# Merging the blocks of a chunk inverse with zero-masked operands on all 128 rows

## The chip, the cores and the metric

The kernel runs on one core of one Trainium2 chip. The metric is the device time of one execution in microseconds; the time of the kernel before is the median of three runs.

## The reference

Two layers of a block over 512 tokens (256 of context, 256 latent): neighbourhood attention and a gated delta rule side by side, then an MLP. The part that matters here belongs to the delta rule. For each chunk, head and direction a unit lower triangular matrix is inverted:

```python
kb = kc * bc[..., None]
a = jnp.where(strict, jnp.einsum('nbhid,nbhjd->nbhij', kb, kc) * decay, 0.0)
tinv = unit_lower_inverse(a)          # (I + a)^-1
u = tinv @ (vc * bc[..., None])
w = tinv @ (kb * eg[..., None])
...                                   # then a scan over the chunks
```

The reference uses chunks of 64 tokens; the kernel works with tiles of 128 tokens, which gives the same recurrence. A layer then has 4 tiles t, 2 directions d and 4 heads: 32 matrices of 128x128, numbered n = 8t + 4d + h.

## The kernel before

Each layer first computes projections and gates, then the inversion and the scan (`mixer`), then the output projection and the MLP. Products of weights are made of three matmuls each (lines 274 to 276), with the weights split into two parts by ScalarE (`whi`, line 248) and VectorE (`wlo`, line 250).

The strings `ord0` and `ord1` list the pieces of work of a layer; at the X stands the inversion with the scan behind it. The pieces named after the X (attention `a`, lines 696 to 719; projections N, K, Q, Z; the steps `f` of the modulation, line 301) are independent of the inversion. Outside the first stage, which is ordered by hand, a planner decides how the instructions of all pieces are laid on each engine, so that attention and projection matmuls stand between those of the inversion. Each engine then works in that order.

The inversion of a layer goes like this. Lines 809 to 816 make the 32 matrices in `U` (128 partitions, 32 matrices, 128 columns), for each tile t from a product `kk` on TensorE and a decay factor from ScalarE (line 805). Lines 823 and 824 take the four diagonal blocks of 32x32 of every matrix out of `U` and transpose them into `MT`, one block row of 32 partitions at a time. Lines 825 to 833 invert the diagonal blocks by substitution on VectorE, all at once, in `Y`. Line 834 transposes the result, lines 835 and 836 scatter it into `XT`, which has been cleared by GpSimd (line 795), and lines 837 and 838 scatter the other orientation into `U`.

Then come two levels of merging, for each half t2 of 16 matrices (two tiles t). The first level joins pairs of 32x32 blocks to 64x64 blocks: p1 (line 849, tiles of 32x32 in the array, once for each r), copied to `y1` by ScalarE (line 850), then pz (lines 853 and 854), whose results are negated into `U` by VectorE (855) and into `XT` by ScalarE (856). The second level joins the two 64x64 blocks to 128x128: p2 (line 862), copied to `y2` (864), then p3 (867 and 868), negated into `U` (869) or `XT` (870); direction 1 is scaled into `U` at line 871. The contraction of each of these matmuls runs over the 32 or 64 partitions of one block:

```python
for r in range(2):
    for n in range(16):
        PE.matmul(p1[B_[r], n], U[A_[r], n0 + n, B_[r]], XT[A_[r], n0 + n, A_[r]], ...)
    S.activation(y1[B_[r]], p1[B_[r]], AF.Copy)
```

The PSUM tiles of this work come from a ring of three (`sm`), the working tiles in SBUF from a ring of seven (`tr`).

Of the kernel before, what the change touches and what calls it, by code (L numbers as in the profile page):

```python
# [11 lines left out]
F32 = mybir.dt.float32  # L12
# [3 lines left out]
AF = mybir.ActivationFunctionType  # L16
ALU = mybir.AluOpType
AX = mybir.AxisListType
# [158 lines left out]
def body(ctx, tc, a, out, dump=None):  # L177
    nc = tc.nc
    V, S, G, PE, SP = nc.vector, nc.scalar, nc.gpsimd, nc.tensor, nc.sync
    dump = dump or (lambda name, ap: None)  # L180

    P0 = ctx.enter_context(tc.tile_pool(name="P0", bufs=1))
# [5 lines left out]
    def sm(name):  # L188
        return PP.tile([128, 512], F32, name=name, tag="g", bufs=CFG["g"])
# [6 lines left out]
    ident = cst[:, C_ID:C_ID + 128]  # L196
# [6 lines left out]
    mh = P0.tile([128, 8], F32, name="mh")  # L203
    V.memset(mh, -0.5)

    hsel = P0.tile([128, 4], F32, name="hsel")
    tdf = P0.tile([128, 8], F32, name="tdf")
    tdsel = P0.tile([128, 8], F32R, name="tdsel")
# [4 lines left out]
    def late_const():  # L213
        SP.dma_start(cst[:, 128:], a["const"][:, 128:])
        V.tensor_copy(idb, ident)
        r = wraw(None)
        SP.dma_start(r[:, :384], a["masks"])
        V.tensor_copy(mb.rearrange("p a b -> p (a b)"), r[:, :384])
        V.tensor_reduce(hsel, ident.rearrange("p (j c) -> p c j", c=4), axis=AX.X, op=ALU.add)
        t = small([128, 32], "t32", bufs=1)  # L220
        V.tensor_reduce(t, ident.rearrange("p (j c) -> p j c", c=4), axis=AX.X, op=ALU.add)
        V.tensor_reduce(tdf, t.rearrange("p (u c) -> p c u", c=8), axis=AX.X, op=ALU.add)
        V.tensor_copy(tdsel, tdf)

    def small(shape, name, dt=F32, bufs=3):
        return P0.tile(shape, dt, name=name, tag="sm_" + name, bufs=bufs)
# [6 lines left out]
    def wraw(src, name="wraw"):  # L233
        r = P0.tile([128, 1024], F32, name=name, tag="wraw", bufs=4)
        if src is not None:
            r_dma[:] = [SP.dma_start(r, src).ins]
        return r
# [229 lines left out]
    def mixer(l, hT, pre, ctx_m):  # L467
# [3 lines left out]
        M = ctx_m.enter_context(tc.tile_pool(name="mix%d" % l, bufs=1, reuse_waits="tile"))  # L471

        def tr(name, shape=(128, 512), dt=F32, bufs=None):
            return M.tile(list(shape), dt, name=name, tag="tr", bufs=CFG["tr"])
# [8 lines left out]
        U = M.tile([128, 32, 128], F32, name="U", tag="U")  # L483
        XT = M.tile([128, 32, 128], F32, name="XT", tag="XT")
# [106 lines left out]
        beta = g = po = gc = gx = gt = cd = eg = ngc = gcb = neg = kd = None  # L591
# [205 lines left out]
        def decay(t, d, form, bias):  # L797
            pr = sm("gcr").rearrange("p (h c) -> p h c", h=4)
            m = mb[:, "abc".index(form)].unsqueeze(1).to_broadcast([128, 4, 128])
            PE.matmul(pr, idb, m, start=True, stop=False, skip_group_check=True)  # L800
            PE.matmul(pr, tdsel[:, 2 * t + d:2 * t + d + 1].to_broadcast([128, 128]), gx,
                      start=False, stop=True, skip_group_check=True)
            D_ = tr("dec").rearrange("p (h c) -> p h c", h=4)
            for h in range(H):
                S.activation(D_[:, h], pr[:, h], AF.Exp, bias=bias[:, t, 4 * d + h:4 * d + h + 1],
                             scale=-1.0 if form == "c" else 1.0)
            return D_

        for t in ts:
            kk_ = sm("kk").rearrange("p (h c) -> p h c", h=4)  # L810
            for h in range(H):
                kt_ = kqT[h][:, 0, 128 * t:128 * t + 128]
                PE.matmul(kk_[:, h], kt_, kt_, start=True, stop=True)
            for d in range(2):
                D_ = decay(t, d, "a" if d == 0 else "c", gcb)
                V.tensor_tensor(U[:, 8 * t + 4 * d:8 * t + 4 * d + 4], D_, kk_, op=ALU.mult)

        if l == 0:
            dump("U", U)
        q4 = [slice(32 * b, 32 * b + 32) for b in range(4)]  # L820
        MY = M.tile([128, 2, 32, 32], F32, name="MY", tag="my")
        MT, Y = MY[:, 0], MY[:, 1]
        for b in range(4):
            V.transpose(MT[q4[b]], U[q4[b], :, q4[b]].rearrange("p n i -> p i n"))
        S.activation(Y, MT, AF.Copy, scale=-1.0)
        V.memset(Y.rearrange("p a b -> p (a b)")[:, 0:1024:33], 1.0)
        for j in range(1, 31):
# [3 lines left out]
            V.tensor_tensor(tv, MT[:, j + 1:, j:j + 1].to_broadcast([128, m, j]),  # L831
                            Y[:, j:j + 1, 0:j].to_broadcast([128, m, j]), op=ALU.mult)
            V.tensor_tensor(Y[:, j + 1:, 0:j], Y[:, j + 1:, 0:j], tv, op=ALU.subtract)
        V.transpose(MT, Y.rearrange("p i j -> p j i"))
        for b in range(4):
            S.activation(XT[q4[b], :, q4[b]].rearrange("p n i -> p i n"), MT[q4[b]], AF.Copy)  # L836
        for b in range(4):
            V.transpose(U[q4[b], :, q4[b]].rearrange("p n i -> p i n"), Y[q4[b]])

        LT = U  # L840
        for t2 in range(2):
            n0 = 16 * t2
            y1 = tr("y1").rearrange("p (n c) -> p n c", n=16)
            p1 = sm("p1").rearrange("p (n c) -> p n c", n=16)
            pz = sm("pz").rearrange("p (n c) -> p n c", n=16)
            A_, B_ = [slice(64 * r, 64 * r + 32) for r in range(2)], [slice(64 * r + 32, 64 * r + 64) for r in range(2)]
            for r in range(2):
                for n in range(16):
                    PE.matmul(p1[B_[r], n], U[A_[r], n0 + n, B_[r]], XT[A_[r], n0 + n, A_[r]], start=True, stop=True)
                S.activation(y1[B_[r]], p1[B_[r]], AF.Copy)  # L850
            for r in range(2):
                for n in range(16):
                    PE.matmul(pz[A_[r], n], y1[B_[r], n], U[B_[r], n0 + n, B_[r]], start=True, stop=True)
                    PE.matmul(pz[B_[r], n], U[B_[r], n0 + n, B_[r]], y1[B_[r], n], start=True, stop=True)
                V.tensor_scalar(U[A_[r], n0:n0 + 16, B_[r]], pz[A_[r]], -1.0, None, op0=ALU.mult)
                S.activation(XT[B_[r], n0:n0 + 16, A_[r]], pz[B_[r]], AF.Copy, scale=-1.0)
            lo_, hi_ = slice(0, 64), slice(64, 128)
            for t in (2 * t2, 2 * t2 + 1):
                n0 = 8 * t
                p2 = sm("p2").rearrange("p (n c) -> p n c", n=8)  # L860
                for n in range(8):
                    PE.matmul(p2[hi_, n], U[lo_, n0 + n, hi_], XT[lo_, n0 + n, lo_], start=True, stop=True)
                y2 = tr("y2").rearrange("p (n c) -> p n c", n=8)
                S.activation(y2[hi_], p2[hi_], AF.Copy)
                p3 = sm("p3").rearrange("p (n c) -> p n c", n=8)
                for n in range(4):
                    PE.matmul(p3[lo_, n], y2[hi_, n], U[hi_, n0 + n, hi_], start=True, stop=True)
                    PE.matmul(p3[hi_, 4 + n], U[hi_, n0 + 4 + n, hi_], y2[hi_, 4 + n], start=True, stop=True)
                V.tensor_scalar(U[lo_, n0:n0 + 4, hi_], p3[lo_, 0:4], -1.0, None, op0=ALU.mult)
                S.activation(XT[hi_, n0 + 4:n0 + 8, lo_], p3[hi_, 4:8], AF.Copy, scale=-1.0)  # L870
                V.tensor_tensor(U[:, n0 + 4:n0 + 8], XT[:, n0 + 4:n0 + 8],
                                beta[:, t, 4:8].unsqueeze(2).to_broadcast([128, 4, 128]), op=ALU.mult)
        if l == 0:
            dump("LT", U)

# [182 lines left out]
    with tc.tile_pool(name="xin", bufs=1, reuse_waits="tile") as XP, \  # L1058
# [30 lines left out]
        with tc.manual_schedule(engines={nc.tensor.engine}):  # L1089
            for c in CFG["start"]:  # L1090
                i = cnt.get(c, 0)
                cnt[c] = i + 1
                part = range(KPART * i, KPART * (i + 1))
# [20 lines left out]
                else:  # L1114
                    first_block(pre[int(c)], part)
    fetch()
    late_const()
    P0.tile([128, 40], F32, name="pad")
    dump("h0", hT[0].bitcast(F32))
    x1d = P_dram.tile([256, 1024], F32, name="x1d")  # L1120
    for l in range(L):
        with ExitStack() as ctx_m:
            mT = mixer(l, hT, pre, ctx_m)
# [189 lines left out]
```

## Time and profile before

| what | us |
|---|---|
| median of 3 runs | 1299.35 |
| lowest, highest | 1298.74, 1306.26 |
| the profiled execution | 1304.05 |
| its span | 1302.3 |
| TensorE busy in the span | 1234.8 |
| VectorE busy | 875.1 |
| ScalarE busy | 604.6 |

PE is TensorE, PEld its loads of the stationary operand, DVE VectorE, ACT ScalarE, POOL GpSimd. The span runs from the first to the last instruction of the profiled execution. A busy TensorE can run at either of two clocks; the granted clock is given as a share of 2.4 GHz.

### The profile page before, as it was taken

The numbers are of one execution on the slowest core, as the hardware profiler recorded it, in microseconds if no ns is written. First come the engines' busy times: TensorE is split into PE (matmuls) and PEld (weight loads), VectorE is DVE, ScalarE is ACT, GpSimd is POOL, SyncE is SP. The second block draws the span as 40 slices with busy tenths as digits, with TensorE's granted clock in tenths as the row PEclk, the third lists the DMA queues.
The fourth block names the chain that finished last, engine by engine and source line by source line (L and its number), as shares of the span: only waits on it lengthen the run. The fifth ranks groups of instructions, "written<-read, shape, count | busy, mean of one in ns | idle before, by whom it ended". The sixth has DMA issues, their size and how long they took to land.

```text
span 1302.3 us, 20475 instructions
## 1 busy us (share of the span) xinstructions
PE 1234.8 (95%) x7976; PEld 1006.3 (77%) x7976; DVE 875.1 (67%) x1681; ACT 604.6 (46%) x1079; POOL 81.6 (6%) x82
## 2 busy tenths in 40 slices
PE   7999998999999999999999999899979998999997
PEld 3676666988878988777788888675669877788996
DVE  3788695466579955344444488897965668866677
ACT  2554545565555732322322455555454655544552
POOL 0212100001001000000000001221000010000000
PEclk9999995899999999999999999999958999899999
DMA  9613661023255643533532256235720256555552
GB/s 329 213 65 102 211 219 46 17 78 117 79 194 182 225 150 109 165 130 115 164 129 99 97 178 204 72 107 191 235 92 14 85 179 231 199 184 191 186 187 98
DMA packets 62721, 190.93 MB, mean 147 GB/s; under 512 B 7808, under 2 KB 17824, under 8 KB 62624
## 3 DMA queue, kind: packets, MB, share of 16 engines
q1 hardware_dynamic: 62624, 189.62, 44.2%
q8 instruction: 63, 1.03, 0.3%
q14 instruction: 34, 0.28, 0.1%
HBM read 187.46 MB, written 2.13 MB: 146 GB/s over the span
## 4 chain that ended last, share of the span: by engine, by line
PE 71%; DVE 11%; ACT 4%; issue 2%; POOL 1%; DMA 1%; DVEq 0%; ACTq 0%; POOLq 0%
PE pst L274 7%; PE pst L276 7%; PE pst L275 7%; PE pm L274 7%; PE pm L276 7%; PE pm L275 7%; PE pss L716 3%; PE adaps L301 2%; DVE wlo L250 2%; PE pss L696 2%; PE pss L713 2%; PE psn L274 1%; PE psn L275 1%; PE psn L276 1%; ACT XT L836 1%
## 5 line engine op out<-in xcount | busy, mean ns | idle before, releaser
L250 DVE TENSOR_TENSOR wlo<-wraw,whi 128x1024 fp32r<-128x1024 f32 x224 | 274.7, 1228 | 184.7 <-ACT whi L248 184.3
L248 ACT ACTIVATE whi<-wraw 128x1024 fp32r<-128x1024 f32 x224 | 237.0, 1060 | 316.6 <-PE pst L276 168.9
L274 PE MATMUL pm<-hhi,whi 128*128 128x256 f32 (+1 forms) x544 | 176.4, 324 | 0.8 <-ACT whi L248 0.7
L276 PE MATMUL pm<-hhi,wlo 128*128 128x256 f32 (+1 forms) x544 | 174.5, 321 | 0.0
L275 PE MATMUL pm<-hlo,whi 128*128 128x256 f32 (+1 forms) x544 | 174.4, 321 | 0.0
L274 PE MATMUL pst<-whi,ah 128*128 128x512 f32 x384 | 150.0, 391 | 0.0
L275 PE MATMUL pst<-wlo,ah 128*128 128x512 f32 x384 | 149.5, 389 | 0.0
L276 PE MATMUL pst<-whi,al 128*128 128x512 f32 x384 | 149.1, 389 | 0.0
L274 PEld LDWEIGHTS pm<-hhi,whi 128*128 128x128 f32 x544 | 103.5, 190 | 14.4 <-issue 5.8
L276 PEld LDWEIGHTS pm<-hhi,wlo 128*128 128x128 f32 x544 | 103.6, 190 | 7.7
L275 PEld LDWEIGHTS pm<-hlo,whi 128*128 128x128 f32 x544 | 103.6, 190 | 7.3
L274 PEld LDWEIGHTS pst<-whi,ah 128*128 128x128 f32 x384 | 72.1, 188 | 15.6 <-issue 0.8
L276 PEld LDWEIGHTS pst<-whi,al 128*128 128x128 f32 x384 | 72.1, 188 | 14.8
L275 PEld LDWEIGHTS pst<-wlo,ah 128*128 128x128 f32 x384 | 72.1, 188 | 14.7
L274 PE MATMUL psg<-hhi,whi 128*128 128x512 f32 (+1 forms) x216 | 78.2, 363 | 4.6 <-ACT XT L529 2.3
L276 PE MATMUL psg<-hhi,wlo 128*128 128x512 f32 (+1 forms) x216 | 78.0, 362 | 0.2 <-DVE wlo L250 0.2
L275 PE MATMUL psg<-hlo,whi 128*128 128x512 f32 (+1 forms) x216 | 77.8, 361 | 0.0
L531 DVE SCALAR_TENSOR_TENSOR XT<-U,cw,XT 128x512 f32<-128x512 f32 (+1 forms) x96 | 66.9, 728 | 0.5 <-ACT XT L529 0.4
L1191 ACT ACTIVATE ah<-mr 128x256 fp32r<-128x256 f32 (+1 forms) x68 | 33.5, 492 | 65.6 <-DVE mr L1189 65.6
L301 PE MATMUL adaps<-wraw,scT 128*32 128x256 f32 x640 | 56.0, 397 | 4.8 <-DMA wraw<-w_ada 4.6
L229 POOL TENSOR_TENSOR rs<-ve,mh 128x1 f32<-128x1 f32 x12 | 12.5, 1044 | 629.3 <-DVE bmv L394 362.2
L1192 DVE TENSOR_TENSOR al<-mr,ah 128x256 fp32r<-128x256 f32 (+1 forms) x68 | 35.2, 518 | 24.3 <-ACT ah L1191 24.2
(659 smaller groups left out, 2467.4 us busy)
## 6 DMA issues: line engine op xcount, KB each, us to landing
wraw<-w SPq DMA_DIRECT2D x140, 512.0 KB
wraw<-w_ada SPq DMA_DIRECT2D x80, 512.0 KB
wraw<-w_gdn SPq DMA_DIRECT2D x27, 512.0 KB
wraw<-w_out SPq DMA_DIRECT2D x24, 512.0 KB
xa<-w_ada SPq DMA_DIRECT2D x32, 256.0 KB
wraw<-w_vz SPq DMA_DIRECT2D x16, 512.0 KB
wraw<-w_na SPq DMA_DIRECT2D x16, 512.0 KB
lnrow<-lnr SPq DMA_DIRECT2D x8, 512.0 KB
```

The costliest lines, as they stand in the source:

```text
L248: S.activation(hi, r, AF.Copy)
L250: V.tensor_tensor(lo, r, hi.bitcast(F32), op=ALU.subtract)
L274: PE.matmul(o, l[0], r[0], start=start, stop=False)
L275: PE.matmul(o, l[0], r[1], start=False, stop=False)
L276: last_mm[:] = [PE.matmul(o, l[1], r[0], start=False, stop=stop).ins]
L301: PE.matmul(st["ps"][32 * g:32 * g + 32, :256], scT[:, k, :], w[:, 256 * g:256 * g + 256], start=(k == 0), stop=(k == 7), tile_position=(0 ...
L531: V.scalar_tensor_tensor(av, cin[:, sg:, kk:kk + 256], cw[:, b, kk:kk + 1], av, op0=ALU.mult, op1=ALU.add)
L696: PE.matmul(ps[:, :128 * nkt], nqT[hp][:, a2, qs], nkT[hp][i][:, a2, :128 * nkt], start=i == 0, stop=i == 1)
L713: PE.transpose(ps[:, 128 * kt_:128 * kt_ + 128], p_[:, 128 * kt_:128 * kt_ + 128], ident)
L716: PE.matmul(ps[:, 0:65], p_[:, 128 * kt_:128 * kt_ + 128], nv[:, kt_, hd], start=kt_ == 0, stop=kt_ == nkt - 1)
L1191: S.activation(ah, r, AF.Copy)
L1192: V.tensor_tensor(al, r, ah.bitcast(F32), op=ALU.subtract)
```

## The change

The diagonal blocks are gathered by ScalarE into `Y` as soon as the tile t that they belong to has been made, 16 copies a layer of 32 partitions by 256 elements; one transpose on all 128 partitions then makes `MT`. After the substitution the inverses stay compact: `low` is the transposed result in the layout (128, 32 matrices, 32 columns) and `upp` the other orientation.

A mask `keep` (one column for each block row of 32 partitions) makes zeros. `lowz` is `low` with all but one block row cleared, for each half and r; `y1` is the copied p1 with all but one block row cleared, in two versions. With these operands p1, pz, p2 and p3 contract over all 128 partitions; the foreign rows are multiplied by zeros. p1 has tiles of 128x64 in the array, pz of 128x32, p2 and p3 of 128x64. pz computes only the results that are used later: three of four for each matrix. The compact inverses are copied into `XT` and `U` piece by piece between the merging steps (`put_low`, `put_upp`, `put_rest`), and the steps of the two halves stand interleaved in the program. For p3 GpSimd clears the lower half of `y2`.

```diff
+        V.tensor_reduce(keep, ident.rearrange("p (b j) -> p b j", b=4), axis=AX.X, op=ALU.add)
...
         for t in ts:
...
+            for b in range(4):
+                S.activation(Y[q4[b], :, 8 * t:8 * t + 8].rearrange("p i n -> p n i"), U[q4[b], 8 * t:8 * t + 8, q4[b]], AF.Copy)
...
-        for b in range(4):
-            V.transpose(MT[q4[b]], U[q4[b], :, q4[b]].rearrange("p n i -> p i n"))
+        V.transpose(MT, Y)
         S.activation(Y, MT, AF.Copy, scale=-1.0)
...
-        V.transpose(MT, Y.rearrange("p i j -> p j i"))
-        for b in range(4):
-            S.activation(XT[q4[b], :, q4[b]].rearrange("p n i -> p i n"), MT[q4[b]], AF.Copy)
-        for b in range(4):
-            V.transpose(U[q4[b], :, q4[b]].rearrange("p n i -> p i n"), Y[q4[b]])
+        low = MT
+        V.transpose(low.rearrange("p n j -> p j n"), Y.rearrange("p i j -> p j i"))
+        lowz = {}
+        for t2 in range(2):
+            for r in range(2):
+                z = lowz[t2, r] = tr("lowz").rearrange("p (n c) -> p n c", n=16)
+                if t2 == 0:
+                    V.tensor_scalar(z, low[:, 0:16], keep[:, 2 * r:2 * r + 1], None, op0=ALU.mult)
+                else:
+                    S.activation(z, low[:, 16:32], AF.Copy, scale=keep[:, 2 * r:2 * r + 1])
+        upp = M.tile([128, 32, 32], F32, name="upp", tag="upp")
+        V.transpose(upp.rearrange("p n i -> p i n"), Y)
...
+        def merge_p1(t2):
+            n0 = 16 * t2
+            p1 = sm("p1").rearrange("p (n c) -> p n c", n=16)
+            for n in range(16):
+                for r in range(2):
+                    PE.matmul(p1[half[r], n], U[:, n0 + n, half[r]], lowz[t2, r][:, n], start=True, stop=True)
+            y1[t2] = [tr("y1").rearrange("p (n c) -> p n c", n=16) for _ in range(2)]
+            S.activation(y1[t2][0], p1, AF.Copy, scale=keep[:, 1:2])
+            V.tensor_scalar(y1[t2][1], p1, keep[:, 3:4], None, op0=ALU.mult)
+
+        def put_low(t2):
+            for b in (0, 1):
+                S.activation(XT[q4[b], 16 * t2:16 * t2 + 16, q4[b]], low[q4[b], 16 * t2:16 * t2 + 16], AF.Copy)
+
+        def put_upp(t2):
+            for b in (2, 3):
+                V.tensor_copy(U[q4[b], 16 * t2:16 * t2 + 16, q4[b]], upp[q4[b], 16 * t2:16 * t2 + 16])
+
+        def put_rest(t):
+            for b in (2, 3):
+                S.activation(XT[q4[b], 8 * t + 4:8 * t + 8, q4[b]], low[q4[b], 8 * t + 4:8 * t + 8], AF.Copy)
+            for b in (0, 1):
+                V.tensor_copy(U[q4[b], 8 * t:8 * t + 4, q4[b]], upp[q4[b], 8 * t:8 * t + 4])
+
+        def merge_pz(t2):
...
+            for n in range(16):
+                d = n // 4 % 2
+                for r in range(2):
+                    y, u = y1[t2][r][:, n], upp[:, n0 + n]
+                    if r == 1 or d == 0:
+                        PE.matmul(pz[q4[2 * r], n], y, u, start=True, stop=True, tile_position=(0, 64 * r))
+                    if r == 0 or d == 1:
+                        PE.matmul(pz[q4[2 * r + 1], n], u, y, start=True, stop=True, tile_position=(0, 64 * r + 32))
...
+        def merge_p2(t):
...
+                PE.matmul(p2[hi_, n], U[:, n0 + n, hi_], XT[:, n0 + n, lo_], start=True, stop=True)
+            y2[t] = tr("y2").rearrange("p (n c) -> p n c", n=8)
+            G.memset(y2[t][lo_], 0.0)
+            S.activation(y2[t][hi_], p2[hi_], AF.Copy)
+
+        def merge_p3(t):
...
+            for n in range(4):
+                PE.matmul(p3[lo_, n], y2[t][:, n], U[:, n0 + n, hi_], start=True, stop=True)
+                PE.matmul(p3[hi_, 4 + n], U[:, n0 + 4 + n, hi_], y2[t][:, 4 + n], start=True, stop=True)
...
+        for part, i in ((merge_p1, 0), (merge_p1, 1), (put_low, 0), (put_upp, 0), (merge_pz, 0), (put_low, 1), (put_upp, 1), (merge_pz, 1),
+                        (merge_p2, 0), (merge_p2, 1), (put_rest, 0), (merge_p3, 0), (put_rest, 1), (merge_p2, 2), (merge_p3, 1),
+                        (put_rest, 2), (merge_p2, 3), (merge_p3, 2), (put_rest, 3), (merge_p3, 3)):
+            part(i)
```

## Rows read from the trace of the kernel before

**Rows 1.** The page: busy time of the engines; the granted clock by slice

```profile
PE 1234.8 (95%) x7976; PEld 1006.3 (77%) x7976; DVE 875.1 (67%) x1681; ACT 604.6 (46%) x1079; POOL 81.6 (6%) x82
...
PEclk9999995899999999999999999999958999899999
```

**Rows 2.** Windows by stage, both layers: busy time (instructions) by engine, clock, DMA

```profile
core 0: us, PE busy (x) PEld busy (x) DVE busy (x) ACT busy (x) POOL busy (x), PEclk, DMA share, GB/s
134.00:151.00 17.00, 17.00 (x109) 11.58 (x108) 10.24 (x23) 12.40 (x40) 2.22 (x1) 1.00 0.63 201
...
194.00:204.00 10.00, 5.58 (x57) 3.10 (x55) 9.91 (x6) 8.94 (x7) 0.00 (x0) 0.75 0.35 118
198.96:233.10 34.14, 30.75 (x413) 25.37 (x409) 16.38 (x29) 16.25 (x24) 0.00 (x0) 0.50 0.15 48
236.50:240.00 3.50, 3.50 (x33) 2.66 (x32) 1.13 (x6) 1.59 (x4) 0.00 (x0) 0.51 0.00 0
...
944.70:954.70 10.00, 3.04 (x55) 1.94 (x53) 9.90 (x6) 9.16 (x8) 0.00 (x0) 0.76 0.54 185
949.92:984.05 34.13, 28.85 (x392) 24.63 (x390) 17.92 (x33) 15.76 (x23) 1.83 (x1) 0.50 0.12 40
...
153.50:156.60 3.10, 3.10 (x38) 1.53 (x37) 3.09 (x2) 1.20 (x2) 0.00 (x0) 1.00 0.43 96
```

**Rows 3.** Waits of TensorE, 196 to 250 us and 945 to 1000 us

```profile
PE p L849 <- ACT y L850: 3.4, 1, 3.4
PE p L849 <- ACT XT L836: 1.5, 1, 1.5
...
PE p L849 <- ACT y L850: 5.3, 1, 5.3
PE p L849 <- ACT XT L836: 2.3, 1, 2.3
```

**Rows 4.** Timeline, layer 0, VectorE and ScalarE: start, duration, instruction [idle before]

```profile
150.97 8.09 DVE L824 STREAM_TRANSPOSE MY<-U 32x1024 f32<-32x1024 f32 x4
...
193.80 2.10 DVE L834 STREAM_TRANSPOSE MY<-MY 128x1024 f32<-128x1024 f32 x1
195.82 7.72 DVE L838 STREAM_TRANSPOSE U<-MY 32x1024 f32<-32x1024 f32 x4
...
195.99 7.85 ACT L836 ACTIVATE XT<-MY 32x1024 f32<-32x1024 f32 x4 [0.98 <-DVE MY L834]
```

**Rows 5.** Timeline of TensorE: equal work at the low and the full clock

```profile
223.08 1.91 PE L849 MATMUL p<-XT,U 32*32 32x32 f32 x32
...
948.81 1.19 PE L849 MATMUL p<-XT,U 32*32 32x32 f32 x32 [2.26 <-ACT XT L836]
...
209.31 0.63 PE L275 MATMUL psn<-hlo,whi 128*128 128x512 f32 x1
209.74 0.63 PE L276 MATMUL psn<-hhi,wlo 128*128 128x512 f32 x1
...
187.69 0.39 PE L275 MATMUL psn<-hlo,whi 128*128 128x512 f32 x1
187.92 0.39 PE L276 MATMUL psn<-hhi,wlo 128*128 128x512 f32 x1
```

**Rows 6.** Groups of TensorE by form, 198.96 to 239.96 us: busy, mean ns

```profile
L853 PE MATMUL pz<-U,y 32*32 32x32 f32 x128 | 6.9, 225 | 0.0
L854 PE MATMUL pz<-y,U 32*32 32x32 f32 x128 | 6.9, 225 | 0.0
L862 PE MATMUL p<-XT,U 64*64 64x64 f32 x59 | 6.4, 288 | 0.0
L849 PE MATMUL p<-XT,U 32*32 32x32 f32 x104 | 6.2, 234 | 3.4 <-ACT y L850 3.4
...
L867 PE MATMUL p<-U,y 64*64 64x64 f32 x24 | 3.3, 318 | 0.0
```

**Rows 7.** Groups by line, the whole span: forms near the added ones

```profile
L413 DVE TENSOR_SCALAR x<-x,rs,nm 128x512 f32<-128x512 f32 x10 | 5.4, 544 | 0.1
...
L870 ACT ACTIVATE XT<-p 64x256 f32<-64x256 f32 x8 | 3.0, 375 | 0.8 <-DVE U L869 0.7
```

More of the change, by code (lines that the diff above doesn't have):

```diff
@@ L204, in body @@
     V.memset(mh, -0.5)
+    keep = P0.tile([128, 4], F32, name="keep")
     hsel = P0.tile([128, 4], F32, name="hsel")
@@ L807, in decay @@
             return D_
+        q4 = [slice(32 * b, 32 * b + 32) for b in range(4)]
+        MY = M.tile([128, 2, 32, 32], F32, name="MY", tag="my")
+        MT, Y = MY[:, 0], MY[:, 1]
         for t in ts:
@@ L816, in mixer @@
                 V.tensor_tensor(U[:, 8 * t + 4 * d:8 * t + 4 * d + 4], D_, kk_, op=ALU.mult)
+            for b in range(4):
+                S.activation(Y[q4[b], :, 8 * t:8 * t + 8].rearrange("p i n -> p n i"), U[q4[b], 8 * t:8 * t + 8, q4[b]], AF.Copy)
         if l == 0:
             dump("U", U)
-        q4 = [slice(32 * b, 32 * b + 32) for b in range(4)]
-        MY = M.tile([128, 2, 32, 32], F32, name="MY", tag="my")
-        MT, Y = MY[:, 0], MY[:, 1]
-        for b in range(4):
-            V.transpose(MT[q4[b]], U[q4[b], :, q4[b]].rearrange("p n i -> p i n"))
+        V.transpose(MT, Y)
         S.activation(Y, MT, AF.Copy, scale=-1.0)
@@ L840, in mixer @@
         LT = U
-        for t2 in range(2):
+        half = [slice(0, 64), slice(64, 128)]
+        lo_, hi_ = half
+        y1, y2 = {}, {}
+        def merge_p1(t2):
             n0 = 16 * t2
-            y1 = tr("y1").rearrange("p (n c) -> p n c", n=16)
             p1 = sm("p1").rearrange("p (n c) -> p n c", n=16)
-            pz = sm("pz").rearrange("p (n c) -> p n c", n=16)
[L846 to L872, printed above, removed]
@@ new lines, in put_upp @@
+        def put_upp(t2):
[8 more added lines that the diff above has]
+            n0 = 16 * t2
+            pz = sm("pz").rearrange("p (n c) -> p n c", n=16)
+            for n in range(16):
[6 more added lines that the diff above has]
+                        PE.matmul(pz[q4[2 * r + 1], n], u, y, start=True, stop=True, tile_position=(0, 64 * r + 32))
+            S.activation(XT[q4[1], n0:n0 + 16, q4[0]], pz[q4[1]], AF.Copy, scale=-1.0)
+            V.tensor_scalar(U[q4[2], n0:n0 + 16, q4[3]], pz[q4[2]], -1.0, None, op0=ALU.mult)
+            for t in range(2):
+                ns = slice(n0 + 8 * t, n0 + 8 * t + 4)
+                V.tensor_scalar(U[q4[0], ns, q4[1]], pz[q4[0], 8 * t:8 * t + 4], -1.0, None, op0=ALU.mult)
+                ns = slice(n0 + 8 * t + 4, n0 + 8 * t + 8)
+                S.activation(XT[q4[3], ns, q4[2]], pz[q4[3], 8 * t + 4:8 * t + 8], AF.Copy, scale=-1.0)
@@ new lines, in merge_p2 @@
+        def merge_p2(t):
+            n0 = 8 * t
+            p2 = sm("p2").rearrange("p (n c) -> p n c", n=8)
+            for n in range(8):
+                PE.matmul(p2[hi_, n], U[:, n0 + n, hi_], XT[:, n0 + n, lo_], start=True, stop=True)
[3 more added lines that the diff above has]
+        def merge_p3(t):
+            n0 = 8 * t
+            p3 = sm("p3").rearrange("p (n c) -> p n c", n=8)
+            for n in range(4):
+                PE.matmul(p3[lo_, n], y2[t][:, n], U[:, n0 + n, hi_], start=True, stop=True)
+                PE.matmul(p3[hi_, 4 + n], U[:, n0 + 4 + n, hi_], y2[t][:, 4 + n], start=True, stop=True)
+            V.tensor_scalar(U[lo_, n0:n0 + 4, hi_], p3[lo_, 0:4], -1.0, None, op0=ALU.mult)
+            S.activation(XT[hi_, n0 + 4:n0 + 8, lo_], p3[hi_, 4:8], AF.Copy, scale=-1.0)
+            V.tensor_tensor(U[:, n0 + 4:n0 + 8], XT[:, n0 + 4:n0 + 8],
+                            beta[:, t, 4:8].unsqueeze(2).to_broadcast([128, 4, 128]), op=ALU.mult)
```

## The prediction

> **What bounds the kernel now.** I read the page first: TensorE is busy for 95% of the span, and the row of granted clocks is 9 nearly everywhere, but falls to 5 in two slices, the 7th and the 30th of 40 [rows 1]. Each lies in the inversion of one layer, so the question is what that stage costs. The windows by stage answer it [rows 2]. In layer 0, from 198.96 to 233.10 us, TensorE is busy for 30.75 of 34.14 us at a granted clock of 0.50, that is 1.2 instead of 2.4 GHz, and another 3.5 us from 236.5 run at 0.51. In layer 1 it is 28.85 of 34.13 us at 0.50. Ahead of both lie the only thin stretches of the stage: 5.58 of 10.00 us busy, and 3.04 of 10.00. The waits of TensorE say for what: in layer 0 for the copies into XT (1.5 us) and for the copy into y behind them (3.4), in layer 1 the same two with 2.3 and 5.3 [rows 3]; together 12.5 us. The timeline shows why they are so long: the transpose at L834 ends at 195.9, and four copies into XT then hold ScalarE for 7.85 us in a row, with y queued behind them, while four transposes into U hold VectorE for 7.72 [rows 4].
>
> So the stage loses time in two ways. A queue of scattered copies leaves TensorE without work; and all that TensorE does behind it, its own small tiles and the attention and projection work laid between them, goes at half the clock. What TensorE did before the clock fell: a wait of 1.5 us, then a batch of 32x32 tiles, then a wait again. While it stayed low, tiles of 32 and 64 rows stood in among matmuls of 128 rows. In a stretch of tiles of 128 rows and 32 columns with projections around it (153.5 to 156.6) the clock is 1.00 [rows 2].
>
> Since TensorE is the bound before and behind the stage, a microsecond that it saves here should arrive at the end.
>
> **The clock term.** What an instruction costs at either level is read from equal batches [rows 5]: 32 instructions of p1 take 1.91 us at the low clock and 1.19 at the full one, 38% less; the projection's matmuls of 512 columns start 0.43 us apart at the low clock (209.31 and 209.74) and 0.23 apart at the full one (187.69 and 187.92), 46% less. The small tiles of layer 0 between 198.96 and 239.96 are p1 6.2, pz 6.9 (the second pz line runs beside it), p2 6.4 and p3 3.3 us [rows 6], together 22.8 of the 41.0 - 3.4 = 37.6 us that TensorE is busy there, 61%. Of the 30.75 + 3.5 = 34.2 us at the low clock I therefore call 20.8 small tiles and 13.4 other work. At full clock they lose 20.8 x 0.38 = 7.9 and 13.4 x 0.46 = 6.2 us: 14.1. For layer 1 I take the same split of 28.85 us: 17.6 x 0.38 + 11.25 x 0.46 = 11.9. Both layers: **-26.0**, if the clock is full throughout. Whether it is hangs on the new tiles, all of 128 rows by 64 or 32 columns. No row shows such tiles in this stage; the nearest are the 128*32 tiles named above, at 1.00, and the 32*32 ones, at 0.50. I take the former, but leave two stretches like that at 236.5 (3.5 us at half clock) in each layer: 7 us x 0.42 = 2.9 each, **+5.9**. The bounds are 0 and the whole 26.
>
> **The queue ahead of p1.** Instead of four strided copies (7.85 us) p1 needs the compact inverses times the mask: the transpose remains, then two multiplications of 128x512 on VectorE. The same form at L413 takes 544 ns [rows 7], so 1.1 us. The first p1 is ready 6.8 us earlier. The waits of 4.9 us in layer 0 vanish, of the 7.6 in layer 1 0.8 stay: **-11.7**. The scattered writes into XT and U come later, as pieces (put_low, put_upp, put_rest) that lie beside p1 and pz; in layer 0 ScalarE and VectorE are each busy for about 16 of 34 us there [rows 2], which hides them. What is late next is the third transpose (upp, 2.1 us on VectorE, behind the masks), which pz waits for; p1 of both halves stands ahead of it on TensorE, and behind it attention work, so I cost it at nothing; uncovered it is about 1 us in each layer.
>
> **The tiles.** pz leaves out a quarter of its matmuls (48 for 64 in each half). Its 6.9 us are some 4.3 at full clock, a quarter is 1.1, in both layers **-2.1**. p1 now loads 64 columns for 32. From below, it alternates two column positions, as pz does, whose two lines share 6.9 us for 256 instructions (27 ns each); from above it costs as much as p2 with its 64 columns, 6.4 us for 59 (108 ns at the low clock) against 6.2 for 104 (60 ns). That is -2 to +4 us in a layer; I take 0, since the two effects oppose each other. p2 and p3 keep their columns and gain only rows: nothing, as the 128 rows of the projections and the 32 of p1 stream alike; between -1 and +1.
>
> **The gathering.** VectorE's four transposes (8.09 us [rows 4]) become one of 2.1: the substitution could start 6.0 us sooner. But ScalarE gets 16 copies of 32x256 a layer in the stretch of the decays, where it is busy for 12.40 of 17.00 us [rows 2]. One costs between 0.38 us (64x256 at L870 [rows 7]) and 0.5 (a quarter of a strided copy, 7.85 / 16, which scatters in the same way), so 6 to 8 us against 4.6 free: the stretch grows by 1.4 to 3.4 us, and the last group of four copies, some 2 us, follows behind the last product. Net -2.6 to -0.6 a layer. How well the copies fall between the decays' exponentials the trace can't show; a clumsy order costs up to +3. I take +1 a layer, **+2.0**, since work that TensorE has for cover here it lacks later. The memsets of y2 lie on GpSimd, which is busy for 6% of the span [rows 1].
>
> **The rivals.** First, *the low clock has another cause than the rows*, and stays. For it: no row shows tiles of the new forms, and the clock was low for 34 us in which TensorE showed as busy for 30.75. Against it: the first fall came behind a wait. Then only the wait goes, and a quarter of pz at the low clock (3.4 us): -11.7 - 3.4 + 2 = -13, **1286**. By the Trainium skill (TensorE: Matmul & The Clock Gate, Part 1) the clock follows how busy the engine is and comes back after sustained matmuls; by that rule rows would give nothing and 1286 would be the time; the row of 30.75 busy us at 0.50 speaks against busy time alone.
>
> Second, on the other side, *the full rows cost and don't pay*. A matmul over all 128 rows leaves none to a neighbour. If the clock stays at half and p1 costs what p2 does (128 instructions x 48 ns = 6.1 us a layer), and pz's 192 instructions go one after another at the 54 ns that a pair takes now (10.4 for 6.9, +3.5), the stage grows by 9.6 us a layer: +19.2 - 11.7 + 3 for the gathering = +10, **1310**. It decides once the clock stays low and more than 9 us of the 19 are real. Against it: the halves r of p1 and pz are already issued one after another, so no neighbour is lost. The Trainium skill (TensorEngine Tiling (Array Packing), Performance Considerations) asks for row tiling with contractions up to 64, which speaks against padding; by it the lost concurrency could double p1 and pz. No run here shows 32-row tiles above one another.
>
> Third, *the wait moves*: masks, third transpose, y1 on two engines and the gathering leave TensorE waiting as long as before, 12.5 us in all, and the clock still recovers for half the stage: -13.0 - 2.1 + 4 = -11 to -16, about **1285**.
>
> **How the numbers follow.** The sum is -26.0 + 5.9 - 11.7 - 2.1 + 2.0 = -31.9. Against the profiled execution's 1304.05 us this gives 1272; that run lies 4.7 above the median of the timed ones, and the terms are small, so from 1299.35 I forecast **1267**. Chances: forecast 0.67, clock stays 0.15, wait moves 0.11, slower 0.07. Low end: full clock throughout (-26.0), all waits gone (-12.5), pz (-2.1), p1 and gathering at their good ends (-4 and -5.2), -50, of which I allow -48: 1251. High end: it takes in the two rivals at 1285 and 1286 with their costs of up to 4: 1291. Within 1% (13 us, about what a measurement of this kernel tells from none) lies half of the two middle rivals and a little of the second: 0.14; slower by over 1% most of the second, with its copies and waits on top: 0.05; the rest, 0.81, is faster.
>
> **What would show it.** Right: the clock row has at most an 8 where the 5s stand; the waits of TensorE for XT and y are gone; p1, pz and p2 follow the transpose within 10 us; the matmuls of scan and attention start some 15 to 20 us earlier in each layer, and the stages behind have their old lengths. Clock rival: 0.50 still stands over the new p1 and pz. Second rival: p1 instructions over 100 ns apart. Third: TensorE waits for masks, upp or gathered Y. Wrong from outside the sum: a planner that lays out the attention or projection work otherwise, or weight loads that come too late once TensorE is faster.

## The result, and the profile after

The changed kernel takes 1281.85 us (median of 4 runs, 1279.77 to 1283.33) against 1302.64 for the kernel before on the same chip: a ratio of 0.9836, 95% interval 0.9801 to 0.9871. It is 21 us faster where 32 were forecast; 1267 would have been 0.975 of the 1299.35 that the forecast started from. Its profiled execution took 1283.33 us.

The page after, busy times and the granted clock by slice:

```profile
PE 1211.8 (95%) x7848; PEld 989.4 (77%) x7848; DVE 860.4 (67%) x1706; ACT 618.7 (48%) x1131; POOL 86.2 (7%) x90
...
PEclk9999997999999999999999999999979999999999
```

The 5s of [rows 1] have become 7s: the low clock is shorter, not gone. The windows after show how long it lasts, and what it is like before it; columns as in [rows 2]:

```profile
140.00:160.00 20.00, 16.28 (x101) 11.07 (x99) 6.37 (x9) 19.12 (x44) 0.00 (x0) 1.00 0.53 177
188.00:199.00 11.00, 8.71 (x51) 6.46 (x49) 10.19 (x24) 5.27 (x8) 0.00 (x0) 1.00 0.34 101
199.08:212.73 13.65, 12.04 (x294) 10.87 (x296) 10.06 (x21) 8.36 (x18) 2.59 (x4) 0.51 0.11 45
932.00:943.00 11.00, 7.52 (x72) 5.43 (x70) 10.35 (x23) 6.37 (x10) 0.00 (x0) 1.00 0.64 216
943.10:956.70 13.60, 12.74 (x323) 11.80 (x324) 9.80 (x24) 7.70 (x18) 2.59 (x4) 0.51 0.03 9
```

The stretches of 34 us in [rows 2] are now 13.7 us in each layer. New is the first line: in the decays ScalarE is busy for 19.12 of 20 us, and TensorE has work for only 16.28. The waits of TensorE, 132 to 250 us and 870 to 1000 us (total, times, longest):

```profile
PE p L860 <- DVE lowz L844: 4.0, 1, 4.0
PE kk L818 <- ACT dec L807: 2.5, 2, 1.2
PE pvt L590 <- ACT vT L587: 1.3, 1, 1.3
...
PE p L860 <- DVE lowz L844: 4.2, 1, 4.2
...
PE pvt L590 <- ACT vT L587: 2.4, 1, 2.4
PE kk L818 <- ACT dec L807: 2.1, 2, 1.1
```

p1 waited 12.5 us for XT and y [rows 3] and now waits 8.2 for masks; the four lines on decays and values (8.3 us) are waits for the busy ScalarE, of which the kernel before had only 0.9 us, for vT in layer 1. The timeline of ScalarE, VectorE and, last, TensorE in layer 0 shows both causes; where [rows 4] had transposes, the gathering and one transpose stand now:

```profile
156.89 2.65 ACT L823 ACTIVATE MY<-U 32x256 f32<-32x256 f32 x4 [0.26 <-DVE U L821]
...
159.58 1.25 DVE L827 STREAM_TRANSPOSE MY<-MY 128x1024 f32<-128x1024 f32 x1 [2.72 <-ACT MY L823]
161.99 0.17 DVE L834 TENSOR_TENSOR btmp<-MY 128x30 f32<-128x30 f32 x1 [1.17 <-issue]
...
196.62 1.99 DVE L838 STREAM_TRANSPOSE MY<-MY 128x1024 f32<-128x1024 f32 x1
198.48 1.89 DVE L848 STREAM_TRANSPOSE upp<-MY 128x1024 f32<-128x1024 f32 x1
200.22 0.80 DVE L844 TENSOR_SCALAR lowz<-MY,keep 128x512 f32<-128x512 f32 x2
...
200.69 7.42 PE L860 MATMUL p<-lowz,U 128*64 128x32 f32 x128 [3.99 <-DVE lowz L844]
```

The last group of four copies (L823) ends at 159.54, and only then comes the transpose. And the transpose into upp (L848) stands ahead of the masks (L844), not behind them as I had assumed. Against that, the masks are cheaper than reckoned, 0.40 us each for 0.54. And the clock falls at 199.3, while TensorE still waits: the first p1 starts at 200.69. In layer 1 it likewise falls ahead of p1, which starts at 943.96. So here no new tile has run yet when the clock goes down.

**Splitting a time into clock and work.** Every run lists its span and its mean clock. Since the clock has two levels, 2 x (1 - clock) x span is the time spent at the lower one: 2 x 0.020 x 1281.6 = 51 us after, 2 x 0.037 x 1302.3 = 96 before. Within each kernel, runs differ in it (before from 72 to 121 us), and the time follows: over 89 runs of the 12 kernels of this study, with each kernel's mean taken out, a microsecond at the low clock costs 0.39 us (correlation 0.96). So each mean time can be parted into 0.39 times its low time and a rest, which is what the time would be at full clock. The rest is steady, with deviations of 1 to 2 us within a kernel.

| kernel | median, us | ratio to before, 95% | mean, us | at low clock, us | rest, us |
|---|---|---|---|---|---|
| before (33 runs) | 1299 to 1304 | | 1303.3 | 94 | 1266.6 |
| the changed kernel | 1281.85 | 0.9836 [0.9801, 0.9871] | 1281.7 | 52 | 1261.2 |
| e1_rows | 1287.22 | 0.9900 [0.9862, 0.9938] | 1289.4 | 73 | 1261.0 |
| e2_gather | 1269.39 | 0.9755 [0.9710, 0.9799] | 1270.5 | 41 | 1254.4 |
| e3_masks | 1281.49 | 0.9841 [0.9815, 0.9867] | 1281.7 | 47 | 1263.2 |
| e4_fill | 1275.54 | 0.9800 [0.9766, 0.9835] | 1276.4 | 24 | 1267.2 |
| e5_gather_rows | 1283.71 | 0.9819 [0.9756, 0.9881] | 1283.4 | 71 | 1255.6 |
| e6_fill_rows | 1293.64 | 0.9887 [0.9833, 0.9941] | 1292.3 | 66 | 1266.7 |
| e7_before_fill | 1304.89 | 1.0003 [0.9958, 1.0047] | 1306.1 | 74 | 1277.1 |
| e8_gather_fill | 1269.07 | 0.9729 [0.9681, 0.9777] | 1269.0 | 32 | 1256.4 |
| e9_gather_masks | 1265.97 | 0.9682 [0.9632, 0.9732] | 1265.6 | 32 | 1253.3 |
| e10_gather_masks_fill | 1262.74 | 0.9680 [0.9645, 0.9714] | 1262.4 | 18 | 1255.6 |

One of the ten runs of e7 (1318.31 us) was a slow one; without it the mean is 1304.8 us, the low time 72 and the rest 1276.8.

The change itself: 41.7 us less at the low clock (-16.3 us), and a rest that is 5.4 us less. All experiments but e7 are edits of the changed kernel.

### The profile page after: what moved, and what is told of

Read it like the earlier page. It is cut to its first block, busy times and chain, and to the rows that moved or that the text cites. A ratio compares the mean times of both kernels' runs of the same rounds, so it can differ in the third digit from the quotient of the medians.

```text
span 1281.6 us, 20315 instructions
## 1 busy us (share of the span) xinstructions
PE 1211.8 (95%) x7848; PEld 989.4 (77%) x7848; DVE 860.4 (67%) x1706; ACT 618.7 (48%) x1131; POOL 86.2 (7%) x90
## 4 chain that ended last, share of the span: by engine, by line
PE 71%; DVE 9%; ACT 4%; issue 3%; DMA 2%; POOL 2%; DVEq 0%; ACTq 0%; POOLq 0%
PE pst L276 8%; PE pst L277 8%; PE pst L278 8%; PE pm L276 7%; PE pm L278 7%; PE pm L277 7%; PE pss L718 3%; DVE wlo L252 2%; PE adaps L303 2%; PE pss L698 2%; DMA wraw<-w_ada 1%; PE pss L715 1%; PE psn L276 1%; ACT MY L823 1%; PE psn L277 1%
## 5 line engine op out<-in xcount | busy, mean ns | idle before, releaser
L303 PE MATMUL adaps<-wraw,scT 128*32 128x256 f32 x640 | 51.2, 391 | 5.8 <-DMA wraw<-w_ada 5.6
L231 POOL TENSOR_TENSOR rs<-ve,mh 128x1 f32<-128x1 f32 x12 | 12.5, 1044 | 630.7 <-DVE bmv L396 362.2
```

The lines of the kernel that those rows point to most:

```text
L303: PE.matmul(st["ps"][32 * g:32 * g + 32, :256], scT[:, k, :], w[:, 256 * g:256 * g + 256], start=(k == 0), stop=(k == 7), tile_position=(0 ...
```

## The experiments

**Rows alone (e1).** My theory: zero-masked operands over 128 rows hold the clock up. The rival: only the waits matter. The same matmuls, contracting over the 32 or 64 rows that aren't zero; in p1 for instance

```diff
-                    PE.matmul(p1[half[r], n], U[:, n0 + n, half[r]], lowz[t2, r][:, n], start=True, stop=True)
+                    PE.matmul(p1[half[r], n], U[q4[2 * r], n0 + n, half[r]], lowz[t2, r][q4[2 * r], n], ..., tile_position=(64 * r, 64 * r))
```

> The changed kernel with one thing undone: p1, pz, p2 and p3 contract only over the 32 or 64 partitions that aren't zero; masks, order and copies stay. Theory (the rows of the tiles bring the clock back): the granted clock stays at 0.50 for some 27 to 34 us of each layer's merging, as before the change, instead of 13.7 us; the time rises by 9 to 16 us over the changed kernel (1291 to 1298). Rival (the clock comes back because the stage has become shorter and denser, whatever the rows): low clock for 14 us again, time within 3 us of the changed kernel.

Measured: 5.4 us slower in the median, 7.7 in the mean, though with a wide spread (1281 to 1297 us) and ratio intervals that just overlap; that is between the theory's 9 to 16 and the rival's 3. The rest is the same to 0.2 us; the difference is 21 us more at the low clock. So 128 rows cost nothing as such, and they do act on the clock, but in this kernel only by a part.

**Gathering undone (e2).** The four transposes of before take the place of ScalarE's 16 copies:

```diff
-            for b in range(4):
-                S.activation(Y[q4[b], :, 8 * t:8 * t + 8].rearrange("p i n -> p n i"), U[q4[b], 8 * t:8 * t + 8, q4[b]], AF.Copy)
...
-        V.transpose(MT, Y)
+        for b in range(4):
+            V.transpose(MT[q4[b]], U[q4[b], :, q4[b]].rearrange("p n i -> p i n"))
```

> The changed kernel with the gathering undone: the diagonal blocks are taken by four transposes of 32 partitions on VectorE, as before the change. Theory (the 16 copies fill ScalarE and delay the decays): TensorE's waits for the decays and for vT (8.1 us in both layers together) go, the substitution starts 1 to 3 us earlier in each layer, the time falls by 3 to 8 us (1274 to 1279). Rival (the transposes hold VectorE for 8 us, so that one delay replaces the other): within 2 us of the changed kernel.

Measured: 12.5 us faster in the median, more than the 3 to 8 expected. The row of clocks, the waits for the masks in both layers, the timeline and the stretch of the decays, of this kernel:

```profile
PEclk8999999999999999999999999899889999999999
```

```profile
PE p L859 <- DVE lowz L843: 1.5, 1, 1.5
...
PE p L859 <- DVE lowz L843: 2.0, 1, 2.0
```

```profile
147.73 8.00 DVE L826 STREAM_TRANSPOSE MY<-U 32x1024 f32<-32x1024 f32 x4
...
157.04 0.20 DVE L833 TENSOR_TENSOR btmp<-MY 128x30 f32<-128x30 f32 x1
...
194.75 0.30 PE L859 MATMUL p<-lowz,U 128*64 128x32 f32 x2 [1.47 <-DVE lowz L843]
195.54 3.92 PE L859 MATMUL p<-lowz,U 128*64 128x32 f32 x126
```

```profile
140.00:160.00 20.00, 19.15 (x129) 12.30 (x127) 15.42 (x23) 8.81 (x24) 0.00 (x0) 1.00 0.61 208
```

Four transposes of 2 us on VectorE, which had the time, are better than one of 1.25 behind 10.8 us of copies on ScalarE: the substitution starts at 157.04 instead of 161.99, and p1 5.9 us sooner. TensorE's other work ends at 193.28 instead of 196.70 (start of p1 less the wait), only 3.4 us sooner, so the wait ahead of p1 is 2.5 us shorter. In layer 0 the clock is full through the merging; in layer 1, behind a wait of 2.0 us, it is low for 6.8 us of it. Of the 11.2 us of the means the rest is 6.8 and the clock 4.4.

**Masks first (e3).** The transpose into upp is held until the masks are issued, and the copies into XT likewise on ScalarE:

```diff
+        with tc.issue_after(m_dve):
+            V.transpose(upp.rearrange("p n i -> p i n"), Y)
```

> The changed kernel, with the third transpose (upp) queued on VectorE behind the two masks of the first half and the copies into XT queued on ScalarE behind the masks of the second half. Theory (p1 waits because upp was placed ahead of its masks): TensorE's wait for lowz falls from 4.0 and 4.2 us to some 2.3 each, the time by 2 to 5 us (1277 to 1280); if that wait alone brings the clock down, the merging runs at full clock and the time falls by 9 to 12 us. Rival (pz then waits for upp instead): within 2 us.

Measured: no change. The wait for the masks went, and another came, in layer 0 and in layer 1:

```profile
PE psn L276 <- DVE KL L757: 2.9, 1, 2.9
...
PE psn L276 <- DVE KL L757: 3.1, 1, 3.1
```

The projections, TensorE's work beside the inversion, need VectorE to empty their PSUM tile into KL. In layer 0 that instruction (198.25 us) is queued behind the transpose at L838 (196.16 to 198.22), and the projection that needs it now stands ahead of p1 on TensorE, so that p1 starts at 199.72, only 1.0 us sooner than in the changed kernel. The wait isn't the masks' alone: TensorE waits for whatever VectorE does last there.

**Work added ahead of p1 (e4).** Does the clock fall because of the wait, or because of the new tiles? Five matmuls of 128x512 a layer, whose result isn't used, were meant to fill the wait:

```diff
+        for i in range(5):
+            PE.matmul(fl, Yf[:, 0:128], Yf[:, 0:512], start=True, stop=True)
```

> The changed kernel with work added whose result isn't used: in each layer five matmuls of 128x128 by 512 in fp32 (some 0.85 us each) that need the finished substitution, ahead of p1 in the program. Theory (the new tiles hold the clock and only the wait ahead of them brings it down): p1 starts at a full clock and p1 and pz stay at it, the low clock in the merging falls from 13.7 us to at most 4 in each layer; of the 8.5 us that the matmuls cost, the clock gives most back, so that the time lies within 5 us of the changed kernel. Rival (the narrow tiles bring the clock down themselves, whatever their rows): it falls during p1 all the same, the time rises by 6 to 9 us.

Measured: 6.3 us faster in the median, with ratio intervals that overlap, although 9.1 us of work were added. The row of clocks, where the added matmuls ran in layer 0, and p1 and pz by form:

```profile
PEclk9999999999999999999999999999999999999999
```

```profile
173.70 4.56 PE L853 MATMUL fill<-MY 128*128 128x512 f32 x10
```

```profile
L864 PE MATMUL p<-lowz,U 128*64 128x32 f32 x128 | 4.2, 223 | 1.3 <-DVE lowz L844 1.3
L891 PE MATMUL pz<-upp,y 128*32 128x32 f32 x96 | 2.6, 198 | 0.6 <-DVE y L867 0.6
```

The matmuls did not run where I wanted them. They read only the first half of `Y`, which is ready in the middle of the substitution, and TensorE did them there, 23 us ahead of p1. What changed in the wait came about another way: projection work moved behind them, VectorE has 4 emptyings into KL (L757) for 7 in its queue ahead of the transpose at L838, which starts at 192.62 for 196.62, and p1 starts at 196.98 for 200.69, behind a wait of 1.3 us for 4.0. The profiled run is also the one of the four with the least low time: 13 us by its mean clock, where the others have 18, 31 and 33; each run of the changed kernel has 51 to 54.

In the changed kernel, then, it is the wait that brings the clock down; tiles of 128 rows behind a wait of 1.3 us did not in this run. That a shorter wait can be enough is seen also in layer 0 of e2, which has no added work.

**Rows where the wait is short (e5, e6).** e5 is e2 with the 32- and 64-row operands of e1, e6 is e4 with them.

> The kernel with the gathering undone (e2_gather), and p1, pz, p2 and p3 contracting over their 32 or 64 partitions only. Theory (with the wait ahead of p1 short, the full rows are what keeps the clock): the low clock in the merging grows by 7 us or more in each layer over e2_gather's 0 and 13.7, the time by 4 to 10 us (1273 to 1279). Rival (the waits alone set the clock; the rows are worth nothing): within 2 us of e2_gather, 1267 to 1272.

> The kernel with added matmuls ahead of p1 (e4_fill, full clock through both mergings), and p1, pz, p2 and p3 contracting over their 32 or 64 partitions only. Theory (tiles of 32 and 64 rows bring the clock down without any wait): it falls within p1 or pz, 7 us or more low in each layer, time up by 4 to 10 us over 1275.5. Rival (only waits bring it down): full clock, time within 2 us.

Measured: e5 is 14.3 us slower than e2, e6 18.1 slower than e4. Both are more than the 4 to 10 us expected. The rests differ by 1.2 and -0.5 us; the low clock by 30 and 42 us. The intervals of the ratios overlap for e5 and e2 and touch for e6 and e4, but each run of e5 and e6 is slower, and longer at the low clock, than every run of its partner. The windows of e6:

```profile
190.00:200.00 10.00, 8.63 (x71) 6.71 (x72) 9.21 (x21) 5.75 (x11) 0.00 (x0) 1.00 0.28 99
200.00:217.10 17.10, 17.10 (x334) 15.10 (x331) 7.52 (x21) 8.96 (x20) 2.59 (x4) 0.50 0.01 2
```

and the same stretches of e4, with the same wait of 1.3 us in it:

```profile
190.00:200.00 10.00, 8.74 (x114) 7.11 (x113) 7.94 (x17) 5.05 (x10) 0.20 (x1) 1.00 0.14 49
200.00:217.00 17.00, 16.35 (x402) 13.98 (x399) 12.73 (x31) 14.03 (x31) 2.11 (x4) 1.00 0.01 3
```

TensorE is as busy ahead of 200 us in both, and busier behind it in e6. In the kernels' text only the rows differ, and the clock is 0.50 against 1.00.

**The kernel before with its waits filled (e7).** Nine unused matmuls a layer, on MT, where p1 waited for the copies into XT:

```diff
+        for i in range(9):
+            PE.matmul(fl, Mf[:, 0:128], Mf[:, 0:512], start=True, stop=True)
```

> The kernel before the change with nine matmuls of 128x128 by 512 in fp32 added in each layer (some 7.7 us, result unused) where TensorE waits for the copies into XT. Theory (the tiles of 32 and 64 rows lower the clock themselves): the merging starts at full clock but runs low for 20 us or more of the 40 in each layer; what the filled wait gives back is small, 1295 to 1305. Rival (the wait alone brought the clock down): full clock through the merging; -26 for the clock, +3 for what the matmuls exceed the waits by, 1275 to 1285.

Measured: no gain. The windows of layer 0:

```profile
196.00:206.00 10.00, 10.00 (x88) 5.50 (x90) 9.10 (x10) 7.88 (x6) 0.00 (x0) 1.00 0.00 0
206.00:221.70 15.70, 15.36 (x370) 12.16 (x366) 9.75 (x23) 9.74 (x19) 0.00 (x0) 1.00 0.22 70
221.75:238.80 17.05, 17.05 (x161) 14.52 (x161) 6.13 (x17) 5.86 (x11) 1.83 (x1) 0.50 0.19 55
```

In this layer the waits are filled (in layer 1, 3.0 us are left), and the clock stays full for longer (it fell at 199 before). But it falls all the same, at 221.7, among tiles of 32 and 64 rows with attention work between them, and TensorE was idle for only 0.34 of the 25.7 us before. The low time is 20 us less (-7.7), which the added matmuls cost again (rest +10.5).

**Gathering undone and work added (e8).** e2 with two unused matmuls a layer. As in e4 they ran in the substitution (at 168 us in layer 0), not between it and p1.

> The changed kernel with the four transposes on VectorE in place of the gathering, and two matmuls of 128x512 per layer whose result isn't used, between the substitution and p1. Question: did the gathering cost through the clock alone, or also through waits in the decays? The clock should be full throughout, as with five such matmuls and the gathering (1275.5). Clock alone: only the three matmuls fewer count (2 x 3 x 0.91 = 5.5 us), about 1270. Waits too (5.5 us for the masks' neighbours: the waits for dec and vT, 8.3 us in the changed kernel, vanish): about 1264, low stretches under 4 us in both layers.

Measured: 1269.07, as clock alone would have it, but for another reason: the clock was not full (17 us low in the merging of the profiled run, behind waits of 1.4 and 0.9 us). The rest tells more: 1256.4 against 1267.2 with five matmuls and the gathering. Three matmuls fewer a layer are at most 5.5 of these 10.8 us; at least 5.3 are the gathering's waits. So it costs by both ways, as e2 had it.

**Gathering undone and masks first (e9), and with the fill (e10).** e9 is e2 with e3, e10 adds the two matmuls to it.

> The kernel with the gathering undone (e2_gather) and upp queued behind the masks (e3_masks). Theory (the wait ahead of p1 shortens by 2 us in each layer, and with it the clock of the second layer stays up): 1262 to 1267. Rival (the wait moves on to the work that VectorE does behind upp, as in e3_masks): within 2 us of e2_gather's 1269.4.

> As the fastest version so far (transposes on VectorE, masks first: 1266.0), with two unused matmuls of 128x512 per layer between the substitution and p1. If the wait ahead of p1 is what brings the clock down in layer 1 (10.2 us low), the low stretches vanish (-10.2 x 0.42 = -4.3), the matmuls cost 3.6 and fill at most 2.6 of waits: about 1263 to 1264. If the clock falls there because of the waits for weights earlier (3.7 us for adaps), the stretches stay and the time is 1267 to 1269.

Measured: e9 is 3.4 us faster than e2 in the median; their ratio intervals overlap a little, so the order of the masks is probably worth something here, but it isn't settled. In e10 no low stretch is left in either merging:

```profile
PEclk9999999999999999999999999899999998999999
```

Its rest rises by 2.3 and its low time falls by 14 us. Its median is 3.2 us under that of e9, its ratio the same, so the two can't be told apart. Both are faster than either kernel: without a wasted matmul, e9 takes 0.968 of the time before, which is 16 us less than the changed kernel.

## Why the prediction was right in direction and too high in gain

The time lies in the range, but near the high end, which had been put there for the two rivals at 1285 and 1286; the time alone doesn't tell the forecast from them. Of the signs named, the waits for XT and y are gone and the scan of layer 0 starts 18.1 us earlier (223.9 for 242.0), but the 5s became 7s and not 8s, p1 runs at 0.51, and TensorE waits for masks, which was the third rival's sign. That the chain of reasons (wait, low clock, rows) held is known from the experiments; the sum of -31.9 was 11 too much. A further 3 us of the miss of 15 is the start at 1299.35, where the kernel before then gave 1302.64. The steps of the sum, by their own numbers:

- **The gathering, "I take +1 a layer, +2.0": the step that failed.** Against VectorE's transposes it costs 11.2 us, 9 more than forecast, and with them in its place the change is worth -32.8 (means of e2 and before), the sum forecast; it divides into -20.6 for the clock and -12.2 for the rest, where -20.1 and -13.8 were forecast without the gathering. I had bounded a copy by 0.38 and 0.5 us; it takes 0.66 (2.65 / 4). So ScalarE got 10.8 us a layer, not 6 to 8, where 4.6 were free, and TensorE waits there for decays and values. I had said that TensorE lacks later what it has for cover here, and priced that at nothing beyond the stretch's own growth: the later substitution lengthened the wait ahead of p1, and that wait holds the clock down.
- **The queue, -11.7.** Waits of 0.8 us were to stay; 8.2 did. "What is late next is the third transpose (upp, 2.1 us on VectorE, behind the masks)" was wrong in the order: it went ahead of them. But e3 shows that the order alone gives nothing. Without the gathering 3.5 us stay, in e9 2.6.
- **The clock, -26.0 + 5.9.** Its price was right: I took 0.42 for a microsecond at the low clock, the runs give 0.39. Its extent was off: 7 us were to be left in each layer, 13.7 were, and 3.4 more in layer 1. That followed from the waits, as far as the profiled runs show it: with them short, nothing was low in the mergings of e4 and e10, 7 us in each of e2 and e9 (and 7 and 3 us ahead of the merging in layer 1), but 17 us in e8.
- **The tiles, -2.1 and 0.** p1 in e2 takes 31 ns an instruction at the full clock (3.92 / 126), no more than the 37 of [rows 5] (1.19 / 32, a shorter batch, so that its last instruction weighs more). pz takes 2.6 us for the 4.3 that I had estimated, less by more than the quarter. Full rows cost nothing: e1, e5 and e6 have the rests of their partners within 1.2 us.

The rivals. *Another cause than the rows* is refuted where the wait is short (e5, e6) and half true where it isn't: in the changed kernel the clock falls in the wait whatever the rows, and fewer rows cost only 5 to 8 us more. By the Trainium skill (TensorE: Matmul & The Clock Gate, Part 1) the clock depends on how busy the engine is. The windows of e6 and e7, at 0.50 with 17.10 of 17.10 and 17.05 of 17.05 us busy, show that a busy time in the trace isn't enough for it. *Full rows cost and don't pay* is refuted: with full rows no rest is higher by more than 0.5 us, although p1's tiles of 32 rows alternate between two row positions in e1, e5 and e6. The Trainium skill (TensorEngine Tiling (Array Packing), Performance Considerations) asks for row tiling with contractions up to 64. Here that gains nothing in work and loses 12 to 17 us by the clock (30 and 42 us x 0.39) where the wait is short. *The wait moves* came nearest in time, with 1285. All waits of TensorE listed for the two stretches are 20.5 us before and 19.2 after, so they did move, to the masks, the decays and the values; the clock recovered 41 of the 72 low us in the merging.

What stays open: why the clock fell in e8 behind waits of 1.4 and 0.9 us and not in e4 behind 1.3 and 1.5, nor in layer 0 of e2 behind 1.5. Each is a single profiled run, and the runs of one kernel differ in their low time (e4 from 13 to 33 us, e8 from 23 to 38), so it can be the chance of a run. What TensorE had done just ahead differs as well, and no run separates the two; how short a wait must be is not shown. How the chip judges a tile of 32 rows is also not shown, only that the clock falls on it.

## What to carry to other kernels

Price a wait on TensorE twice, once by its length and once by the low clock that follows, and part a measured time into the two with each run's clock: here 0.39 us for a microsecond at half clock, and a rest that moves only with the work. Padding a contraction with zero rows cost nothing and held the clock up: it was worth 5 to 8 us behind the long wait and 14 to 18 where the wait was short. Before work goes over to an idle-looking engine, count it with the strided form's own price in the stretch where it will run: 10.8 us where 4.6 were free gave back a third of this gain. And look in the trace where added work ran: the matmuls of e4 ran 23 us ahead of the wait that they were to fill.

## What the runs showed of the hardware

- The clock fell in the middle of dense work with 32- and 64-row tiles, with 0.34 us idle in the 25.7 us before (e7, at 221.7 us), and stayed at 1.00 on the same products with 128 rows (the profiled run of e4).
- The 32x32-block transpose of 128x1024 took 1.25 us between unpermuted operands (L827), 1.89 to 1.99 with one or both permuted (L848, L838), and 2.0 for 32 partitions of 1024 elements that are permuted and read out of `U` in runs of 32 (8.00 / 4): fewer partitions gained nothing here, and a permuted access cost 0.6 to 0.7 us.
- A ScalarE copy of 32x256 that gathers and permutes blocks took 0.66 us, more than the 64x256 of [rows 7] with 0.375, which writes runs of 64.
